# Gated-DeltaNet/Conformer mixer of a decoder step: the work between the recurrence's steps put into one pinned stream, its head in a pool of its own, tanh for sigmoid and silu, states updated on VectorE

## The chip, the cores and the metric

One core of one Trainium2 chip runs the whole program. The metric is the device time of one execution in microseconds (us), the median of three runs. TensorE is called PE here, VectorE DVE, ScalarE ACT, GpSimd POOL, SyncE SP, as in the profile.

## What is computed

One inference step of a two-layer decoder for 256 prompt tokens and 8 sample tokens, which share weights and stand side by side as T = 264 columns. The change concerns the first layer's mixer and the norms; the mixer cut to what matters is:

```python
proj = h @ p['ab_w_in']                       # q,k,v | z | b,a | ga,gb
qkv, new_dn_conv = causal_depthwise_conv(qkv_raw, dn_conv, p['dn_conv_w'])   # 4 taps
q, k, v = split(silu(qkv));  q = l2_normalize(q) * 128**-0.5;  k = l2_normalize(k)
beta = sigmoid(b_raw);  g = -exp(A_log) * softplus(a_raw + dt_bias)
o, new_S = gated_delta_rule(q, k, v, g, beta, dn_S)      # chunks of 64, 4 heads of 128
o = rms_norm(o, p['dn_norm_g']) * silu(z)
glu = ga * sigmoid(gb)
c, new_cc_conv = causal_depthwise_conv(glu, cc_conv, p['cc_conv_w'])         # 31 taps
c = silu(layer_norm(c + p['cc_conv_b'], p['cc_ln_g'], p['cc_ln_b']))
y = concatenate([o, c], -1) @ p['ab_w_out']
```

The delta rule needs, for each chunk and head, the inverse of a unit lower triangular 64x64 matrix. Every sample token has a state of its own, 4 heads of 128x128, that is decayed and gets an outer product of key and value. Around the mixer stand feed-forward layers, cross-attention to 256 memory tokens (whose keys and values are projected here too) and a layer norm after each.

## The kernel before

Activations lie transposed (channels on partitions, tokens in columns), and float32 products are made of three: a weight is split into `whi` (a cast on ACT, L224) and `wlo` (a subtraction on DVE, L217), and high times high, low times high and high times low are added. So a projection works by **units** of 128 output columns; a unit's 24 matmuls (8 blocks of 128 rows, 3 each) are called products (`Unit.products`, L700). Weights come in blocks of 128x8x256 ("raw", 1 MB, three buffers) on SP's queue.

The Tile framework's scheduler sets each engine's order by the program's dependences and the order of writing; an instruction marked by `pin` (`keep_in_program_order`) stays where it is written. An engine runs its list in order: an instruction that waits holds up all behind it.

The mixer (`mixer`, L868) goes through these steps:

- `Norm.finish` ends the feed-forward's norm while the query and key units are projected; `ev_qkv` (L911) copies each unit to `qkvraw` and makes the 4-tap convolution: an ACT multiplication (L916) and three DVE steps of 128x256 (L918). Sample tokens get their taps on POOL from transposed state rows (`conv_states`, tiles stn, dsn, dsT). Silu of four groups at once is at L934.
- **Head of the recurrence**: b and a are projected (`pba`), turned (`pbt`) and give beta and the decay gv by a chain of small ACT and DVE steps (L1006 to L1032). Sums of squares of keys and queries (`sq`, L1078 and L1081) give the l2 norms, `br2` and, after a Newton root (`rsqrt`, L125 to L131), `nk`. The running decay is spread by an all-ones product of `tg` = tri times gv (8 ACT multiplications, L1115, one matmul a chunk half, L1119); with it DT, NT (keys by keys) and AT (queries by keys) are made. The 256 tokens are two halves of 128, c = 0 and 1.
- **Levels**: five doubling levels (L1263 on) invert 32x32 blocks for both halves. In a level a half needs np (DVE), a product of X (L1278), a transposition of XP, a product of XT (L1286), a subtraction on DVE and four copies to X (L1247), each waiting for the one before. Two larger levels (32 to 64, 64 to 128) follow; then the halves are run through (`vn,XT`, L1350, to the state S). The sample tokens' states are read twice: once for key and query times state (`S_s,kq`, L1203), once in `update`.
- **What fills the gaps** is written after the recurrence: the gated units ga and gb (`glu`), the 31-tap convolution as 32 matmuls for each of 4 groups (`taps`, L972), the z units (`zeta`), `conv_norm`, and four units of the next attention's keys (`fill`). Nothing of that is pinned; the scheduler draws it forward into gaps that it foresees. The value units are projected ahead of the head.
- **End**: `update` multiplies each of 8 state blocks by its decay on ACT (L1464) and adds the outer product 128x512 at a time on DVE (L1469), four times; `og` is the normed output times z; then the output projection begins, whose first products need the split of `og` (xlo, L187).

ACT holds one set of function tables; an `ACT_TABLE_LOAD` stands where the next function is not in it. The mixer has ten.

## Time and profile before

| | us |
|---|---|
| three runs, lowest / median / highest | 1386.66 / 1388.01 / 1389.65 |
| the profiled execution | 1386.02 |
| its span, from first to last instruction | 1384.3 |
| PE busy in the span | 1345.3 (97%) |
| DVE busy | 938.5 (68%) |
| ACT busy | 747.5 (54%) |
| POOL busy | 200.1 (14%) |

The mixer lies between 248 us (the transposition of stn) and 408 us (the output projection's first product). "Busy" counts the time in which at least one instruction of the engine is under way; "granted clock" (PEclk) is the mean share of full speed in a stretch, and the clock has two levels, 2.4 and 1.2 GHz, so 0.90 is a fifth of the stretch at the lower one. In a timeline a row joins like instructions that follow each other: its start, its duration, their count, and in brackets how long the engine had been idle before and what ended the wait. Matmul records of float32 operands other than the split ones come twice for one matmul.

### The profile page before, as it was taken

To read this page: it belongs to the slowest core of one execution; us is meant where nothing else is said; L and a number is where in the kernel's file an instruction comes from. 1 tells how busy PE (TensorE), PEld (TensorE's weight loads), DVE (VectorE), ACT (ScalarE), POOL (GpSimd) and SP (SyncE) were. 2 spreads that over 40 slices of the span, in tenths; PEclk is the share of its full clock that TensorE was granted. 3 is DMA by queue.
4 is the path that set the end of the run, shared out by engine and by line. 5 is a ranking of instruction groups with operands and counts; after the bars stand their busy time and mean duration, and the time that the engine had idled before them with its cause. 6 is when DMAs were issued, how large, how long until landed. Compare 5 with 4: busy or idle time off the path is not lost. (4 is left out here: it accounts for less than half of the span.)

```text
span 1384.3 us, 27373 instructions
## 1 busy us (share of the span) xinstructions
PE 1345.3 (97%) x10959; PEld 1272.9 (92%) x10959; DVE 938.5 (68%) x1910; ACT 747.5 (54%) x1372; POOL 200.1 (14%) x242
## 2 busy tenths in 40 slices
PE   8999999988989999999999999999999999999998
PEld 8999999865879978999999999999999968999997
DVE  5555668865658776975556865556888987855554
ACT  4455447774555644664445654445766635744443
POOL 3312410301111000111121011121112001011021
PEclk9999999999989999999999999999999999999999
DMA  7654766436569988455556755555648993665551
GB/s 261 216 165 159 242 193 183 142 109 152 179 186 313 290 279 258 152 176 181 184 176 195 211 172 181 179 174 182 192 147 273 287 299 119 189 203 183 175 169 53
DMA packets 270543, 269.27 MB, mean 195 GB/s; under 512 B 8243, under 2 KB 266291, under 8 KB 270400
## 3 DMA queue, kind: packets, MB, share of 16 engines
q1 hardware_dynamic: 257392, 260.94, 59.7%
q10 hardware_dynamic: 13024, 6.59, 1.9%
q8 instruction: 86, 1.41, 0.4%
q14 instruction: 41, 0.34, 0.1%
HBM read 252.81 MB, written 15.26 MB: 194 GB/s over the span
## 5 line engine op out<-in xcount | busy, mean ns | idle before, releaser
L217 DVE TENSOR_TENSOR wlo<-raw,whi 128x1024 fp32r<-128x1024 f32 (+1 forms) x380 | 460.9, 1220 | 247.5 <-ACT whi L224 244.3
L224 ACT CAST whi<-raw 128x1024 fp32r<-128x1024 f32 (+1 forms) x380 | 389.1, 1030 | 412.9 <-PE mm L700 221.9
L700 PE MATMUL mm<-xhi,whi 128*128 128x264 f32 x1728 | 495.5, 288 | 5.3 <-ACT whi L224 5.2
L700 PE MATMUL mm<-xhi,wlo 128*128 128x264 f32 x1728 | 495.9, 288 | 3.2 <-DVE wlo L217 3.2
L700 PE MATMUL mm<-xlo,whi 128*128 128x264 f32 x1728 | 494.3, 287 | 0.1
L700 PEld LDWEIGHTS mm<-xhi,whi 128*128 128x128 f32 x1728 | 327.5, 190 | 10.1 <-ACT whi L224 6.7
L700 PEld LDWEIGHTS mm<-xhi,wlo 128*128 128x128 f32 x1728 | 326.4, 189 | 8.9 <-DVE wlo L217 4.4
L700 PEld LDWEIGHTS mm<-xlo,whi 128*128 128x128 f32 x1728 | 328.2, 190 | 2.9 <-issue 1.4
L857 PE MATMUL mm<-hh,whi 128*128 128x264 f32 x704 | 200.8, 285 | 0.0
L858 PE MATMUL mm<-hl,whi 128*128 128x264 f32 x704 | 200.4, 285 | 0.0
L859 PE MATMUL mm<-hh,wlo 128*128 128x264 f32 x704 | 200.1, 284 | 0.0
L857 PEld LDWEIGHTS mm<-hh,whi 128*128 128x128 f32 x704 | 132.6, 188 | 0.1
L858 PEld LDWEIGHTS mm<-hl,whi 128*128 128x128 f32 x704 | 132.3, 188 | 0.1
L859 PEld LDWEIGHTS mm<-hh,wlo 128*128 128x128 f32 x704 | 132.4, 188 | 0.0
L187 POOL TENSOR_TENSOR hl<-sg,hh 128x264 fp32r<-128x264 f32 x44 | 61.2, 1392 | 444.8 <-ACT hh L180 444.8
L700 PE MATMUL mm<-xpre,whi 128*128 128x266 f32 x640 | 117.1, 290 | 0.9 <-ACT x L455 0.6
L700 PEld LDWEIGHTS mm<-xpre,whi 128*128 128x128 f32 x640 | 97.9, 189 | 2.1 <-ACT x L455 0.7
L700 PE MATMUL mm<-xpre,wlo 128*128 128x266 f32 x320 | 85.1, 287 | 0.0
L380 POOL TENSOR_TENSOR lnQ<-lnQ,lnsq 128x264 f32<-128x264 f32 x40 | 40.5, 1012 | 298.3 <-ACT lnsq L373 298.2
L806 DVE TENSOR_TENSOR sg<-mm,sg 128x264 f32<-128x264 f32 x76 | 32.9, 432 | 51.3 <-PE mm L700 49.8
L700 PEld LDWEIGHTS mm<-xpre,wlo 128*128 128x128 f32 x320 | 57.7, 189 | 0.1
L1660 DVE CUSTOM_DVE_ANT_0 junk<-cache,ax 128x256 f32<-128x256 f32 x128 | 47.2, 412 | 4.8 <-PE ax L1655 4.6
(492 smaller groups left out, 1775.4 us busy)
## 6 DMA issues: line engine op xcount, KB each, us to landing
raw<-in_ffn_w_gate_dram SPq DMA_DIRECT2D x43, 1024.0 KB
raw<-in_ffn_w_up_dram SPq DMA_DIRECT2D x43, 1024.0 KB
raw<-in_ffn_w_down_dram SPq DMA_DIRECT2D x32, 1024.0 KB
cache<-in_cache_mem_k_dram SPq DMA_DIRECT2D x32, 512.0 KB
cache<-in_cache_mem_v_dram SPq DMA_DIRECT2D x32, 512.0 KB
raw<-in_ffn_w_down_dram SPq DMA_DIRECT2D x16, 768.0 KB
raw<-in_ab_w_in_dram SPq DMA_DIRECT2D x12, 1024.0 KB
raw<-in_xa_wk_dram SPq DMA_DIRECT2D x8, 1024.0 KB
```

The source lines that it names most:

```text
L187: e.tensor_tensor(out=lo, in0=src, in1=f32(hi), op=ALU.subtract)
L217: e.tensor_tensor(out=lo[:, :nk], in0=r, in1=f32(hi[:, :nk]), op=ALU.subtract)
L224: A.copy(hi[:, :nk], r)
L380: pin(e.tensor_tensor(out=Q, in0=Q, in1=sq, op=ALU.add), last)
L700: pin(PE.matmul(self.ps, lhsT=self.w[q // 2][:, k, :], rhs=self.rhs[q % 2][:, k, :], start=self.n == 1, stop=self.n == 3 * KT), pinned)
L806: V.tensor_tensor(out=sg, in0=pu, in1=sg, op=ALU.mult)
L857: PE.matmul(ps, lhsT=hi[:, k, :], rhs=xh, start=n == 0, stop=False)
L858: PE.matmul(ps, lhsT=hi[:, k, :], rhs=xl, start=False, stop=False)
L859: PE.matmul(ps, lhsT=lo[:, k, :], rhs=xh, start=False, stop=n == FT - 1)
L1660: V.tensor_tensor_reduce(out=junk, in0=kc[:, b, a, :], in1=pq[:, b * 256:(b + 1) * 256], scale=1.0, scalar=0.0, op0=ALU.mult, op1=ALU.add, ...
```

## The change

The changed mixer computes the same. `values`, `stream`, `f` and `TE` are new:

- A generator `stream` holds the four value units, gb and ga units, z units and the taps in a fixed sequence; `f(n)` takes the next n matmuls of it, and stands between the recurrence's steps. `TE` pins the recurrence's matmuls too, so PE's order from the head on is the written one.
- The head (ss, br2, DT, NT, AT, eG) moves ahead of the value units, with tiles in a pool `ge`. The values are turned (`values(c)`) in levels 1 and 2.
- In a level the first products of both halves stand together with 8 matmuls of the stream behind each, then the second products with 8 behind each.
- `pg` is made by 4 matmuls with gv broadcast as the stationary operand; the `tg` multiplications go. Sigmoid and the values' silu go by tanh (the conv weights are halved once, and one DVE step 128x1056 multiplies th + 1 by the halved value); gb gets a second ACT step. z's multiplication by dng on POOL is folded into DVE steps.
- A state is updated by 8 DVE steps of 128x128 that multiply by the decay and add the outer product; two of the four state blocks stay in the buffers of the first reading. `vb` is made by 8 ACT multiplications, before by 2 on POOL.
- `conv_norm` is filled with products of key units. Before, five key units were made in the mixer, one ahead of the head and four at the end; now four are, all at the end, and one (24 products and its transpositions) moves to the norm that ends the next attention.
- Small norm tiles become slices of two blocks of 128x3xT, which the taps' input uses later in place of a raw buffer. The raw loads that this frees go on SP's queue earlier: one stands ahead of the load of dsn.

```diff
+        class TE:
+            def matmul(*a, **k):
+                pin(PE.matmul(*a, **k))
...
-                if 1:
-                    o = qkv[i]
-                A.activation(out=o, in_=o, func=AF.Silu)
+                if i < 2:
+                    A.activation(out=o, in_=o, func=AF.Silu)
+                else:
+                    th = cp.tile([P, 4, T], F32, name="th")
+                    A.activation(out=th, in_=o, func=AF.Tanh)
+                    V.scalar_tensor_tensor(out=o, in0=th, scalar=1.0, in1=o, op0=ALU.add, op1=ALU.mult)
...
-            A.activation(out=gbt[n], in_=ps, func=AF.Sigmoid)
+            A.activation(out=gbt[n], in_=ps, func=AF.Tanh, scale=0.5)
+            A.activation(out=gbt[n], in_=gbt[n], func=AF.Identity, scale=0.5, bias=half)
...
+            seq = [(1024, 8, ev_qkv), (1280, 10, ev_qkv), (2056 + 512, 0, ev_gb), (2056, 0, ev_ga), (2056 + 768, 2, ev_gb), 10,
+                   (2056 + 256, 2, ev_ga), 11, (1536, 0, ev_z), 12, (1536 + 256, 2, ev_z), 13]
...
+        def f(n):
+            for _ in range(n):
+                next(fill_in, None)
...
-        fill(0, 1)
-        proj(ab_w_in, 1024, 4, rhs, lambda n, ps: ev_qkv(8 + n, ps))
...
         for c in range(2):
+            f(8 + 4 * c)
+            pg = ax_ps()
             for h in range(H):
-                if 'AAAAAAAA'[4 * c + h] == 'A':
-                    A.mul(tg[:, h, :], tri, gv[:, c, h:h + 1])
...
-            PE.matmul(pg, lhsT=ones[1], rhs=tg.rearrange("p h i -> p (h i)"), start=True, stop=True)
+                TE.matmul(pg[:, h * P:(h + 1) * P], lhsT=gv[:, c, h:h + 1].broadcast_to([P, P]), rhs=tri, start=True, stop=True)
...
         for l in range(5):
...
                     A.copy(xt, pt[:, :P])
-                    px = ax_ps()
...
+                f(8)
+            for c in range(2) if l else ():
+                px = ax_ps()
+                for b in range(4):
+                    TE.matmul(px[32 * b:32 * b + 32, :P], lhsT=xts[c][:, 32 * b:32 * b + 32], rhs=XT[c][:, b, :], start=True, stop=True)
+                V.tensor_tensor(out=XP[c], in0=XP[c], in1=px[:, :P], op=ALU.subtract)
                 spread_blocks('VVVV', X[c], XP[c])
...
+                f(8)
+            if l in (1, 2):
+                values(l - 1)
...
-            S_s = gp.tile([P, 8, P], F32, tag="S_s", name="S_s2", bufs=2)
-            A.dma_start(S_s, S_in[:, 8 * g:8 * g + 8, :])
-            for i in range(8):
-                A.mul(S_s[:, i, :], S_s[:, i, :], eb[:, 0, 2 * g + i // 4, i % 4:i % 4 + 1])
+            S_s = held[g]
+            if g < 2:
+                S_s = gp.tile([P, 8, P], F32, tag="S_s", name="S_s2", bufs=2)
+                A.dma_start(S_s, S_in[:, 8 * g:8 * g + 8, :])
...
-                V.tensor_tensor(out=S_s[:, 4 * a:4 * a + 4, :], in0=S_s[:, 4 * a:4 * a + 4, :], in1=hd(po), op=ALU.add)
+                for h in range(4):
+                    V.scalar_tensor_tensor(out=S_s[:, 4 * a + h, :], in0=S_s[:, 4 * a + h, :], scalar=eb[:, 0, 2 * g + a, h:h + 1],
+                                           in1=hd(po)[:, h, :], op0=ALU.mult, op1=ALU.add)
...
+        keys = kv_units(0, 4)
+        conv_norm(Filler(keys))
+        for n in range(2):
+            update(n)
```

ACT's order has four table loads in the mixer (ten before). PE's order counts as follows, from the transposition of stn to the output projection's first product (products of the 16 projected units, products of key units, taps):

| stretch of the program | before | after |
|---|---|---|
| stn to the first product of pg | 216 products, 24 key products | 48 products |
| pg to the first level's first product | 4 products | 65 products |
| there to `vn,XT` | 110 products, 64 taps | 148 products, 32 taps |
| there to the end of the recurrence (`pr,ones` of the sample tokens) | 6 products, 17 taps | 27 products, 5 taps |
| there to the output projection | 48 products, 47 taps, 96 key products | 96 products, 91 taps, 96 key products |

**ACT, from the silu of keys and queries (tiles keys and mixs) to the squares of the queries.** Before, in two pieces:

```order
L934 ACTIVATE keys<-keys 128x1056
L934 ACTIVATE mixs<-mixs 128x1056
L1006 ACT_TABLE_LOAD
L1006 ACTIVATE beta<-BA 128x12
L1012 ACTIVATE se<-sx 128x12
```

```order
L934 ACT_TABLE_LOAD
L934 ACTIVATE mixs<-mixs 128x1056
L944 ACT_TABLE_LOAD
L944 ACTIVATE gb<-mm 128x264
L1078 ACTIVATE sq<-keys 128x512 x2
L1177 ACT_TABLE_LOAD
L1177 ACTIVATE egs<-gv 8x4
L1078 ACTIVATE sq<-mixs 128x512 x2
```

After, in one:

```order
L954 ACTIVATE keys<-keys 128x1056
L954 ACTIVATE mixs<-mixs 128x1056
L1127 ACTIVATE sq<-keys 128x512 x2
L224 CAST whi<-raw 128x1024
L1080 ACTIVATE beta<-BA 128x12
L1085 ACTIVATE se<-sx 128x12
L937 COPY qkvraw_2573<-mm 128x264
L1086 ACT_TABLE_LOAD
L1086 ACTIVATE se<-se 128x12
L1088 ACTIVATE eA<-eA 128x4
L938 ACTIVATE mixs<-mm,par 128x256
L1093 ACT_TABLE_LOAD
```

The squares stand right behind the silu of keys and queries; the first value unit's cast and copy stand between the steps of the decay's chain, and the values' silu has left this stretch.

**DVE, the last part of the head, up to the first level's np.** Before:

```order
L1142 COPY wl<-DT 128x4
L1150 TENSOR_TENSOR vn<-ax,nk 128x512 x2
L1126 TENSOR_TENSOR DT<-ax,mneg 128x512
L1144 TENSOR_TENSOR eG<-eG,mixs 128x512
L1266 TENSOR_TENSOR np<-NP,pmask 128x128
L1169 TENSOR_SCALAR kq_3593<-ax 128x64
L1273 TENSOR_TENSOR np<-id_101,np 128x128
```

After (mixs is here the value tile; th its tanh):

```order
L1175 SCALAR_TENSOR_TENSOR NT<-ax,br_3293,DT 128x128 x4
L1182 TENSOR_TENSOR AT<-ax,DT 128x512
L1184 COPY wl<-DT 128x4
L217 TENSOR_TENSOR wlo<-raw,whi 128x1024
L940 SCALAR_TENSOR_TENSOR mixs<-qkvraw_2573,par,mixs 128x256 x3
L959 SCALAR_TENSOR_TENSOR mixs<-th,mixs 128x1056
L1231 COPY kq<-keys 128x32
L1232 COPY kq<-mixs 128x32
L1248 TENSOR_TENSOR dg<-ident,beta 8x32
L1235 TENSOR_TENSOR kq_3571<-kq 128x64
L1238 TENSOR_SCALAR kq_3571<-ax 128x64
L1337 TENSOR_TENSOR np<-NP,pmask 128x128
```

The values' convolution, their silu and a weight's low part now stand ahead of np; vn has moved behind it.

**PE, the end of the mixer** (o_nat is the recurrence's output, csq the conv norm's squares, vb,k the outer products of the states). Before:

```order
L1392 MATMUL mm<-mixs,ones_86 128x264 x4
L1428 MATMUL ax<-ident,o_nat 128x128 x8
L1450 MATMUL ax<-ident,kv_4959 128x128 x2
L1399 MATMUL mm<-ones_80,csq 128x1 x12
L1468 MATMUL ax<-vb,k_4971 128x512 x8
L140 MATMUL mm<-dg,ones_80 128x264
```

After:

```order
L710 MATMUL mm<-mlo,whi 128x256
L710 MATMUL mm<-mhi,wlo 128x256
L887 MATMUL ax<-vb,k_4475 128x512 x4
L740 MATMUL mm<-ident,kvT 128x128 x4
L1554 MATMUL ax<-ident,o_nat 128x128 x3
```

The output's transposition, ahead of the conv norm's squares before, now stands behind the last outer products and the key units.

## Rows read from the trace of the kernel before

**Rows 1.** The profile's page, part 1: busy time of PE, its share of the span, instructions.

```profile
PE 1345.3 (97%) x10959; PEld 1272.9 (92%) x10959; DVE 938.5 (68%) x1910; ACT 747.5 (54%) x1372; POOL 200.1 (14%) x242
```

**Rows 2.** The mixer in stretches: from and to in us, length, then busy time (and count of instructions) of PE, PEld, DVE, ACT and POOL, the granted clock, the DMA engines' share and GB/s; the last line adds them up.

```profile
248.00:264.00 16.00, 14.31 (x118) 12.06 (x117) 13.76 (x31) 10.38 (x21) 8.75 (x20) 0.90 0.25 77
264.00:283.00 19.00, 18.58 (x150) 17.92 (x148) 14.45 (x37) 16.64 (x28) 3.98 (x8) 1.00 0.66 201
...
290.00:303.00 13.00, 8.42 (x53) 6.32 (x52) 11.10 (x44) 11.79 (x30) 1.05 (x2) 0.95 0.15 44
303.00:330.00 27.00, 23.84 (x286) 16.05 (x290) 21.88 (x81) 15.14 (x46) 2.47 (x3) 0.90 0.33 90
330.00:352.00 22.00, 18.55 (x299) 14.68 (x290) 3.96 (x22) 8.87 (x24) 2.32 (x3) 0.84 1.04 246
352.00:365.00 13.00, 13.00 (x129) 10.75 (x130) 8.70 (x28) 9.03 (x34) 0.97 (x1) 1.00 0.01 2
...
376.00:391.00 15.00, 12.03 (x59) 8.44 (x58) 11.73 (x31) 4.53 (x11) 5.39 (x4) 0.75 0.72 219
391.00:409.00 18.00, 15.28 (x111) 14.10 (x109) 7.36 (x15) 11.81 (x31) 1.95 (x4) 0.92 0.53 153
sum 161.00, PE 141.81 PEld 114.24 DVE 101.66 ACT 97.26 POOL 27.83; mean PE 14.18 PEld 11.42 DVE 10.17 ACT 9.73 POOL 2.78
```

**Rows 3.** PE's timeline at the borders of the mixer's steps: start in us, duration, engine, line, operation, count, idle time before and what ended it.

```profile
248.52 0.37 PE L893 MATMUL ax<-ident,stn 120*128 120x120 f32 x2
...
283.02 0.43 PE L1081 MATMUL ax<-sq,ones 128*32 128x128 f32 x8 [0.38 <-ACT sq L1078]
...
290.18 0.59 PE L1119 MATMUL ax<-tg,ones 128*128 128x512 f32 x1
...
303.65 0.66 PE L1278 MATMUL ax<-X,np 128*32 128x128 f32 x8 [1.11 <-DVE np L1266]
...
329.48 0.42 PE L1286 MATMUL ax<-XT,xt 128*32 128x128 f32 x8 [0.29 <-ACT xt L1283]
...
330.59 1.91 PE L972 MATMUL mm<-cinx 128*32 128x256 f32 x32
...
338.36 0.64 PE L1203 MATMUL ax<-S_s,kq 128*32 128x128 f32 x16 [1.03 <-DMA S_s<-in_state_dn_S_dram]
...
352.29 0.38 PE L1350 MATMUL ax<-vn,XT 128*128 128x128 f32 x1
...
364.41 0.31 PE L1225 MATMUL ax<-pr,ones 128*128 128x32 f32 x2
...
408.40 0.37 PE L700 MATMUL mm<-xhi,whi 128*128 128x264 f32 x1
```

**Rows 4.** What PE waited for between 248 and 409 us: the line that waits and what ended the wait, total in us, times, longest.

```profile
PE mm L700 <- ACT whi L224: 3.3, 2, 1.7
PE ax L1203 <- DMA S_s<-in_state_dn_S_dram: 3.1, 2, 2.0
...
PE ax L1286 <- ACT xt L1283: 1.8, 6, 0.3
PE ax L1278 <- DVE np L1266: 1.8, 2, 1.1
PE ax L1468 <- DVE S_s L1469: 1.5, 1, 1.5
```

**Rows 5.** ACT's timeline around the silu of keys and queries, and at the squares of the queries.

```profile
261.56 1.08 ACT L934 ACTIVATE keys<-keys 128x1056 f32<-128x1056 f32 x1 [3.94 <-POOL keys L931]
262.55 1.07 ACT L934 ACTIVATE mixs<-mixs 128x1056 f32<-128x1056 f32 x1
263.63 1.28 ACT L1006 ACT_TABLE_LOAD   x1
264.93 0.21 ACT L1006 ACTIVATE beta<-BA 128x12 f32<-128x12 f32 x1
...
284.91 1.14 ACT L1078 ACTIVATE sq<-mixs 128x512 f32<-128x512 f32 x2
...
287.35 0.59 ACT L1083 COPY st<-ax 128x512 f32<-128x512 f32 x1 [1.31 <-PE ax L1081]
```

**Rows 6.** Groups by line between 248 and 409 us, the last two of ACT and the others of DVE: line, engine, operation, tiles, shapes, count, busy us, mean ns of one, idle time before and what ended it.

```profile
L217 DVE TENSOR_TENSOR wlo<-raw,whi 128x1024 fp32r<-128x1024 f32 x21 | 26.6, 1278 | 4.8 <-ACT whi L224 4.8
L918 DVE SCALAR_TENSOR_TENSOR mixs<-qkvraw,par,mixs 128x256 f32<-128x256 f32 x24 | 10.8, 481 | 0.1
...
L1469 DVE TENSOR_TENSOR S_s<-S_s,ax 128x512 f32<-128x512 f32 x8 | 5.3, 678 | 0.9 <-ACT S_s L1464 0.9
...
L1134 DVE SCALAR_TENSOR_TENSOR NT<-ax,br,DT 128x128 f32<-128x128 f32 x8 | 2.4, 350 | 0.2 <-ACT DT L1128 0.2
...
L1150 DVE TENSOR_TENSOR vn<-ax,nk 128x512 f32<-128x512 f32 x2 | 1.4, 688 | 1.3 <-PE ax L1148 1.3
...
L224 ACT CAST whi<-raw 128x1024 fp32r<-128x1024 f32 x20 | 20.6, 1048 | 8.5 <-PE mm L700 4.7 <-DMA raw<-in_xa_wk_dram 3.8
...
L916 ACT ACTIVATE mixs<-mm,par 128x256 f32<-128x256 f32 x4 | 1.9, 482 | 0.0
```

**Rows 7.** PE in a stretch of the following attention, where the moved key unit goes (columns as in Rows 2).

```profile
452.00:465.00 13.00, 13.00 (x110) 13.00 (x110) 7.25 (x12) 8.79 (x14) 0.00 (x0) 1.00 0.93 296
```

**Rows 8.** SP's queue: the issue of the load of dsn.

```profile
251.78 0.34 SPq L899 DMA_DIRECT2D dsn<-in_state_dn_conv_dram  x1
```

More of the change, by code (lines that the diff above doesn't have):

```diff
@@ L275, in turn, with block @@
         return PE.matmul(ps[:, k % 4 * P:(k % 4 + 1) * P], lhsT=t, rhs=ident, start=k % 4 == 0, stop=False, is_transpose=True)
+    def block(name, i):
+        t = work.tile([P, 3, T], F32, tag=f"nb{i}", name=name, bufs=1)
+        return [t[:, j, :] for j in range(3)]
     class Norm:
@@ L969, in taps @@
+        def taps(n, xs, w8):
             pv = mm_ps()
@@ new lines, in mixer @@
+        st = ge.tile([P, 512], F32, tag="AT0", name="st")
+        A.copy(st, pss)
+        f(8)
+        pss = ax_ps()
+        for m in range(4):
+            TE.transpose(pss[:, m * P:(m + 1) * P], st[:, m * P:(m + 1) * P], ident)
+        V.tensor_scalar(out=ss, in0=pss.rearrange("p (i c h r) -> p i c h r", i=2, c=2, h=H)[:, :, :, :, 0], scalar1=1e-6, scalar2=None, op0=ALU.add)
+        br2 = ge.tile([P, 2, H], F32, name="br2")
+        V.reciprocal(out=br2, in_=ss[:, 0])
+        V.tensor_tensor(out=br2, in0=br2, in1=beta[:, 0:2, :], op=ALU.mult)
@@ L1158, in mixer @@
         smp = {}
+        held = {}
         def sample_step():
```

435 lines of the change are left out of this document (232 added, 203 removed).

## The prediction

> **What bounds the kernel now.** I read the page first: PE is busy 97% of the span [rows 1], so a change can gain only where PE idles or runs at the lower clock. The stretches of the mixer show where: of 161.0 us between 248 and 409 PE is busy 141.8, so it idles 19.2, and the granted clock falls to 0.90, 0.84 and 0.75 in stretches around the recurrence [rows 2]. A stretch of 22 us at 0.84 has lost (1 - 0.84) x 22 = 3.5 us of full speed if PE was busy in its slow part; so counted, the stretches shown lost some 13 us in all. Then the border times [rows 3] give five segments: stn to pg 41.7 us (248.5 to 290.2), pg to the first level 13.5, there to `vn,XT` 48.6, there to the end of the recurrence 12.1, there to the output projection 44.0; 159.9 in all. Last the waits [rows 4]: the largest are for weights' casts (3.3) and for the samples' states from DMA (3.1, in front of `S_s,kq`); xt and np, steps within a level, cost 1.8 each. In the first stretches PE is nearly full (18.58 of 19.00), in pg to the first level it is not (8.42 of 13.00), and there DVE is (11.10 of 13.00) [rows 2].
>
> A product costs PE 13.00/110 = 0.118 us where it is full [rows 7], and a tap matmul 1.91/16 = 0.12 (32 records are 16 matmuls) [rows 3]; I take 0.12 for both.
>
> **The change, segment by segment.** PE's work is first moved: 192 products leave segment 1 (240 to 48), -23.0 us; 61 enter segment 2, +7.3; in segment 3 38 more products and 32 fewer taps, +0.7; in segment 4 +21 and -12, +1.1; in segment 5 +48 products and +44 taps, +11.0. The sum is -24 products, the key unit that goes to the attention. What the waits do beside that decides.
>
> *Segment 1, stn to pg.* PE loses what filled it; the end is then set by ACT. The silu of keys waits for POOL as before (3.94 us, starting 261.56), the queries' silu ends at 262.55 + 1.07 = 263.6 [rows 5]. Behind it ACT has in its order: squares of keys 1.14, a cast 1.05 [rows 6], beta and abs 0.2 each, the first value unit's copy (264 columns, where st's 512 take 0.59) 0.4, a table load 1.28, two small exponentials 0.2 each, the unit's convolution step 0.48 [rows 6], a second load 1.28, Ln 0.2, squares of queries 1.14: 7.8, so 271.4. From there PE needs the sums of squares, 16 products (1.9, partly beside), the copy st 0.59 [rows 5] and two transposing steps: 2.6. pg starts at 274.0; the segment has 25.5 us, -16.2. Bounds: 272.5 if the scheduler's pieces fall beside each other, 278.5 if dsn arrives later (its load, issued at 251.78 [rows 8], now stands behind a 1 MB weight load) and the emptied PE falls to the lower clock.
>
> *ACT tables.* Six loads go: by the row of one load, 1.28 with the next activation 0.02 behind its end (263.63 to 264.93) [rows 5], 6 x 1.28 = 7.7 us of ACT, most of it beside PE's work; I count none of it separately. The Trainium skill ("ScalarE: Activation LUTs", section "What ACT_TABLE_LOAD costs") puts a switch at about 2.66 us, load and drain together; the trace shows no such drain, and by the page the two loads left in the head would put pg 2.8 us later than I say.
>
> *Segment 2, pg to the first level.* DVE sets it: 11.10 busy of 13.00 now [rows 2], in a chain. The order puts ahead of the first level's np three low parts at 1.28 (3.8), nine convolution steps of the values at 10.8/24 = 0.45 (4.1), the values' silu step of 1056 columns (not in the trace; twice the 512 columns of 0.68, so 1.3), and takes two vn out (-1.4) [rows 6]: +7.8. The tanh that the silu step waits for stands on ACT ahead of the copies NP, about 1.1 as a silu of the same size [rows 5], and some 0.9 of DVE's 1.9 idle us fills up: 21.5 us, +8.0. Bounds: 18 if most of DVE's added steps fall in waits that the chain has anyway, 25 if each waits for its cast. The four matmuls of pg in place of one (0.59 [rows 3]) and the tg multiplications that go change this by a few tenths either way.
>
> *Segment 3, levels to `vn,XT`.* Four levels with products take 25.8 us now (303.65 to 329.48 [rows 3]); DVE is busy 21.9 of 27 there [rows 2]. It gets some 1.6 more low parts (2.0) and the two vn (1.4): 25.3. PE gets 28 more matmuls (3.4) and loses most of the waits for xt and np. I take 27, with DVE nearly the bound: +1.2. The rest, 22.8 us now, has 21 fewer products (-2.5) and loses the lower clock of 330 to 352 (-3.5) if PE is kept busy before it. The wait for the states, 3.1 [rows 4], I keep for the most part: there are two buffers, so the third and fourth block can be asked for only when the first two have been read, as now, and the next taps' input is loaded at the same time; -1.1. A new one comes: the states' turned products stand right behind their copy on ACT (sT, 512 columns, as st 0.59 [rows 5]), where 16 taps stood between; twice, +1.3. So 17.0, the segment 44.0, -4.6. Bounds: 38 and 49.
>
> *Segment 4.* +1.1 of work, and the seams of eight matmuls wait for vnew and S1 on DVE and ACT: I add 1.3 for two such waits (a 512-column step 0.68 each [rows 6]); 14.5, +2.4, between +1 and +4.
>
> *Segment 5.* Now 44.0. PE idles 3.0 and 2.7 in its last two stretches, and the clock there (0.75 and 0.92) has lost 3.75 and 1.4 [rows 2]: 10.9 that could go (the wait of 1.5 for S_s on DVE [rows 4] is in it), about as much as the 11.0 of work that comes. But new waits come. The output's split stands behind 16 state updates of 128x128 on DVE, 16 x 0.35 = 5.6 us where 4 x 0.68 stood [rows 6], and og, two steps of 512 columns; the first products of the output projection need it, and PE has only 2 to 3 us of transpositions and outer products beside it: 3. vb, now eight ACT steps, has ten taps (1.2) to cover it: 1. So 48.2, +4.2, between 0 and +8. The state multiplications that leave ACT, the two state loads that go and POOL's dng lay beside PE's work: nothing, unless ACT's casts there come sooner.
>
> *The attention* gets 24 products, 2.9, and two transpositions, 0.2. PE is full there (13.00 of 13.00 [rows 7]), so all of it counts: +3.1.
>
> Sum: -16.2 + 8.0 - 4.6 + 2.4 + 4.2 + 3.1 = -3.1. The profiled execution took 1386.0 (its span 1384.3 and 1.7 around it), so it would take 1382.9; the median of the runs stands 2.0 above it, which gives **1384.9**. The rest of the kernel, the norms with their two blocks among it, I leave unchanged: the tiles are the same size, and PE is full beside them.
>
> **The rivals.**
>
> *PE becomes the bound from the first level on* (bigger gain): the two halves' steps overlap so well that DVE's low parts fall between them. Segment 2 at 19.5, segment 3 at 40.0, segment 4 at +1.5, segment 5 at +2.0: -16.2 + 6.0 - 8.6 + 1.5 + 2.0 + 3.1 = -12.2, so 1375.8. For it: DVE was idle 18 of 22 us between 330 and 352 [rows 2], so its work can be spread. Against: in segments 2 and the levels the order holds DVE's steps fixed.
>
> *The waits only move* (the stream does fill the recurrence, but what it fills with was not idle time in the head): the head is a chain on ACT, DVE and POOL with 48 products to cover 25 us, and PE idles there instead. If pg starts at 278.5, segment 1 gains 11.7 in place of 16.2: sum +1.4, so 1389.4, no change. For it: POOL's 3.94 and the ACT chain cannot be shortened by PE's order; against: half of the chain is counted from rows already.
>
> *DVE's order makes it slower*: PE's order is now fixed, so a product whose low part is late holds up the level behind it, where the scheduler before could slip in other work; and DVE has a low part of 1.28 us between the chain's small steps. If a level takes 8.0 us in place of 6.75 (+5.0) and segment 2 24.0 (+2.5), the sum is +4.4, so 1392.4. With that segment 2 it is measurably slower from a level of 7.6 on. For it: DVE at 25.3 of 27 by my own count; against: a level at 6.5 now with DVE 81% busy and the lower clock for a fifth of it.
>
> **How the numbers follow.** The forecast, from -7 to 0 (1381 to 1388), gets 0.42; the larger gain 0.18; waits that only move 0.17; slower 0.23. A measurement of this kernel tells about 0.2% (2.8 us) from no change, so below 1385.2 is faster and above 1390.8 slower. Of the forecast two thirds lie below 1385.2: faster 0.28 + 0.18 = 0.46; same 0.14 + 0.17 = 0.31; slower 0.23. Cases of both signs hold much of the chance, so the range reaches to both: the segments' bounds, taken together at half their widths, go some 10 us either way, 1374 to 1394, and about 0.1 lies on each side (a late head with slow levels above; no new waits in segments 3 and 5 with a quick head below).
>
> **What would show it.** In the changed profile: pg at 274 (278 for the rival of moved waits); the first level's X,np at 295.5, `vn,XT` at 339.5, the end of the recurrence at 354, the output projection at 402. DVE nearly full from pg to the end of the levels, PE's waits there named as np, XP or wlo. A wait of 1 to 3 us for the states in front of `S_s,kq`, and two near 0.6 for sT. In segment 5 a wait of several us for og's low part. If the granted clock is below 0.9 in the head as well as in the levels, I am wrong on the slow side; if levels take 6 us, on the fast side.

## The result, and the profile after

The changed kernel takes 1404.99 us (median of 4 runs, 1402.19 to 1406.38) beside 1388.18 of the kernel before: the ratio is 1.0126, interval 1.0111 to 1.0140. It is 17 us slower where 3 us less were forecast, and above the range. The profiled execution took 1402.19, its span 1400.5.

The stretches between the same border points as before (from the first transposition of stn to pg, the first level's product, the states' first product, `vn,XT`, the end of the recurrence, and the norm after the output projection; columns as in [rows 2]):

```profile
247.40:277.40 30.00, 17.31 (x130) 13.69 (x129) 19.33 (x52) 16.02 (x32) 9.17 (x21) 0.72 0.28 84
277.40:299.10 21.70, 15.32 (x133) 14.59 (x134) 19.17 (x60) 13.21 (x33) 3.63 (x8) 0.95 0.36 107
299.10:328.40 29.30, 28.11 (x275) 22.06 (x275) 22.46 (x80) 17.11 (x51) 0.43 (x1) 0.92 0.48 134
328.40:346.50 18.10, 14.64 (x286) 11.55 (x286) 4.86 (x21) 8.26 (x23) 3.11 (x4) 1.00 0.62 180
346.50:359.50 13.00, 13.00 (x111) 12.06 (x110) 10.15 (x33) 4.30 (x16) 0.00 (x0) 1.00 0.09 26
359.50:448.20 88.70, 80.72 (x660) 68.29 (x660) 55.66 (x148) 39.99 (x78) 6.80 (x13) 0.94 0.68 210
sum 200.80, PE 169.10 PEld 142.25 DVE 131.63 ACT 98.89 POOL 23.14; mean PE 28.18 PEld 23.71 DVE 21.94 ACT 16.48 POOL 3.86
```

The kernel before, counted at the same borders (first and last stretch, and the sum of all six):

```profile
248.52:290.18 41.66, 39.53 (x336) 35.41 (x335) 29.27 (x76) 31.83 (x59) 12.73 (x27) 0.96 0.49 147
...
364.41:437.54 73.13, 67.05 (x523) 58.06 (x522) 51.59 (x124) 39.29 (x81) 13.59 (x14) 0.93 0.79 248
sum 189.02, PE 169.62 PEld 140.63 DVE 125.74 ACT 115.27 POOL 33.13; mean PE 28.27 PEld 23.44 DVE 20.96 ACT 19.21 POOL 5.52
```

PE idles 31.7 of the 200.8 us, where before it idled 19.4 of 189.0: it is busy as long as before (169.1 and 169.6) and idles 12.3 more. The head (first row) has 17.3 busy of 30.0 at a granted clock of 0.72, where before 41.7 us there were nearly full (39.5) at 0.96; pg to the first level 15.3 of 21.7 at 0.95. The levels (third row) are nearly full: 28.1 of 29.3. The last row, 88.7 us, has 8.0 idle and a clock of 0.94; before it was 73.1 with 6.1 idle at 0.93.

Where PE waits between 248 and 425 us, to be read against [rows 4]:

```profile
PE ax L924 <- DMA dsn<-in_state_dn_conv_dram: 5.9, 1, 5.9
PE ax L887 <- ACT sq L1127: 5.6, 2, 5.0
PE ax L887 <- DVE np L1337: 3.7, 2, 3.0
PE ax L887 <- DVE kq L1235: 3.3, 1, 3.3
PE mm L710 <- DVE kvn L741: 2.7, 2, 2.1
PE mm L887 <- DMA cinx<-cin: 2.4, 2, 1.8
PE ax L890 <- ACT sT L1276: 1.8, 2, 1.1
...
```

Of the waits of [rows 4] those for weights' casts, for states from DMA and for xt are gone, and that for the state update is down from 1.5 to 0.9. In their place stand waits of the head: for dsn and for the squares; between pg and the first level for kq and np; and at the end for kvn and for the taps' input (cinx). On PE's timeline, against [rows 3]:

```profile
255.70 1.45 PE L924 MATMUL ax<-ident,dsn 24*128 24x24 f32 x12 [5.92 <-DMA dsn<-in_state_dn_conv_dram]
...
272.20 1.18 PE L887 MATMUL ax<-sq,ones 128*32 128x128 f32 x16 [5.01 <-ACT sq L1127]
...
277.44 0.83 PE L887 MATMUL ax<-tri,gv 128*128 128x128 f32 x6
...
299.06 0.66 PE L887 MATMUL ax<-X,np 128*32 128x128 f32 x8 [3.05 <-DVE np L1337]
...
346.54 0.38 PE L887 MATMUL ax<-vn,XT 128*128 128x128 f32 x2
...
359.55 0.31 PE L887 MATMUL ax<-pr,ones 128*128 128x32 f32 x2
...
419.40 0.36 PE L710 MATMUL mm<-xhi,whi 128*128 128x264 f32 x1 [2.06 <-DVE kvn L741]
```

dsn's load lands where it did, but nothing lies before its transposition now: 5.92 us. The squares of the queries are waited for 5.01 us; pg starts at 277.44. `X,np` waits 3.05 for np and starts at 299.06. `vn,XT` comes at 346.54 (before 352.29), the recurrence ends at 359.55 (364.41). The output projection begins at 414.99 (408.40) with twelve products of the convolution's half, after 0.68 us for a copy kvn (the copy that empties a key unit's accumulator), and waits for another one, 2.06 us, at 419.40.

ACT in the head, against [rows 5]:

```profile
263.62 1.08 ACT L954 ACTIVATE keys<-keys 128x1056 f32<-128x1056 f32 x1 [6.04 <-POOL keys L951]
264.61 1.07 ACT L954 ACTIVATE mixs<-mixs 128x1056 f32<-128x1056 f32 x1
265.58 1.13 ACT L1127 ACTIVATE sq<-keys 128x512 f32<-128x512 f32 x2
...
271.54 1.13 ACT L1127 ACTIVATE sq<-mixs 128x512 f32<-128x512 f32 x2
...
273.45 0.59 ACT L1132 COPY st<-ax 128x512 f32<-128x512 f32 x1 [0.78 <-PE ax L887]
```

The silu of keys starts 2.1 us later than before, again behind POOL. POOL's first step behind the copy dsT, before and after:

```profile
257.33 0.55 POOL L929 TENSOR_TENSOR keys<-dsT,par 128x32 f32<-128x32 f32 x1 [2.33 <-ACT dsT L903]
...
257.73 3.15 POOL L949 TENSOR_TENSOR keys<-dsT,par 128x32 f32<-128x32 f32 x1 [5.17 <-ACT dsT L925]
```

The step starts 0.4 us later and takes 2.6 us more; why it does, no run shows. From the end of the silu of queries (265.68) to the end of the squares of the queries (272.67) ACT runs 7.0 us without a wait, through the steps that the prediction counted at 7.8.

### The profile page after: what moved, and what is told of

It is laid out like the page before. It is cut to its first block, busy times and chain, and to the rows that moved or that the text cites. A ratio compares the mean times of both kernels' runs of the same rounds, so it can differ in the third digit from the quotient of the medians.

```text
span 1400.5 us, 27426 instructions
## 1 busy us (share of the span) xinstructions
PE 1348.5 (96%) x10971; PEld 1277.9 (91%) x10971; DVE 945.7 (68%) x1937; ACT 732.8 (52%) x1338; POOL 190.9 (14%) x239
## 5 line engine op out<-in xcount | busy, mean ns | idle before, releaser
L867 PE MATMUL mm<-hh,whi 128*128 128x264 f32 x704 | 200.8, 285 | 0.0
L869 PE MATMUL mm<-hh,wlo 128*128 128x264 f32 x704 | 200.1, 284 | 0.0
L385 POOL TENSOR_TENSOR lnS<-lnS,lnsq 128x264 f32<-128x264 f32 x40 | 40.0, 1000 | 299.5 <-ACT lnsq L378 299.4
```

The costliest lines, as they stand in the source:

```text
L385: pin(e.tensor_tensor(out=Q, in0=Q, in1=sq, op=ALU.add), last)
L867: PE.matmul(ps, lhsT=hi[:, k, :], rhs=xh, start=n == 0, stop=False)
L869: PE.matmul(ps, lhsT=lo[:, k, :], rhs=xh, start=False, stop=n == FT - 1)
```

## The experiments

Each is the changed kernel with one edit, unless it says otherwise; times are ratios to the kernel before of the same session. One caution on places: the program from the first attention's scores to the end, which no experiment's edit touches, took between 899.9 and 904.4 us in the profiled executions. So differences under some 4 us count here only where the intervals part, and a single trace's place counts only for what is in that place. And the profiled execution of the changed kernel is the fastest of its four (1402.2, its median 1405.0), so a run's gain by its median can be some 3 us more than its places show.

| run | ratio | interval | median us | stn to the norm behind the mixer, us |
|---|---|---|---|---|
| before | 1 | | 1387.2 to 1388.2 | 189.0 |
| changed | 1.0126 | 1.0111 to 1.0140 | 1405.0 | 200.8 |
| e1 dsn early | 1.0126 | 1.0107 to 1.0144 | 1404.4 | 197.0 |
| e2 key unit in head | 1.0064 | 1.0048 to 1.0081 | 1396.9 | 200.0 |
| e3 output early | 1.0097 | 1.0081 to 1.0114 | 1401.7 | 200.9 |
| e4 no pins | 0.9912 | 0.9898 to 0.9927 | 1374.8 | 173.9 |
| e5 stream free | 0.9953 | 0.9937 to 0.9970 | 1381.2 | 179.5 |
| e6 recurrence free | 1.0066 | 1.0046 to 1.0085 | 1396.5 | 196.5 |
| e7 head filled | 1.0047 | 1.0029 to 1.0064 | 1393.9 | 192.5 |
| e8 no pins, e2, e3 | 0.9900 | 0.9884 to 0.9915 | 1373.4 | 175.5 |
| e9 no pins, old update | 0.9907 | 0.9890 to 0.9924 | 1374.5 | 173.5 |
| e10 no pins, no tanh | 0.9928 | 0.9909 to 0.9947 | 1378.6 | 176.7 |
| e11 pins, e2, e3, filled | 1.0030 | 1.0018 to 1.0042 | 1392.0 | 192.1 |
| e12 e8 with dsn early | 0.9930 | 0.9908 to 0.9952 | 1378.1 | 181.1 |
| e13 products without use | 1.0076 | 1.0059 to 1.0093 | 1399.0 | 200.1 |
| e14 keys first | 1.0070 | 1.0055 to 1.0085 | 1398.3 | 197.6 |

### Waits of the head and the end, one by one: e1, e2, e3

```diff
-            dsn = cp.tile([NS * 3, 1536], F32, tag="stn", name="dsn")
-            SP.dma_start(dsn, state_dn_conv.rearrange("b t c -> (b t) c"))
...
+        dsn = cp.tile([96, 512], F32, name="dsn")
+        G.memset(dsn, 0.0)
+        for a in range(3):
+            SP.dma_start(dsn[32 * a:32 * a + 24, :], state_dn_conv.rearrange("b t c -> (b t) c")[:, a * 512:(a + 1) * 512])
```

> The changed kernel with one edit: the 24 state rows dsn get a tile of their own (three blocks of 24 rows, turned by 4 transpositions in place of 12) and their load is issued ahead of that of stn, so that it need not wait for stn's tile nor stand behind a 1 MB weight load. Theory A (the head of the recurrence lost its cover: 192 products left it and PE now stands idle or at the lower clock there): the wait of 5.92 us in front of the transposition of dsn goes, the silu of keys comes 3 to 5 us earlier, pg at about 273 to 275 in place of 277.4, time 3 to 5 us under the changed kernel (about 1400 to 1402). Theory B (the pinned order of products and recurrence is what costs): the head's wait is replaced by another of nearly the same length, gain under 1.5 us.

The ratio is that of the changed kernel. PE's timeline of this run shows why, in two of its rows between 250 and 264 us:

```profile
251.68 0.52 PE L927 MATMUL ax<-ident,dsn 96*128 96x96 f32 x4 [0.28 <-issue]
...
263.01 1.16 PE L887 MATMUL ax<-id,ba 128*128 128x8 f32 x6 [6.89 <-DVE ba L1071]
```

The wait for dsn is gone, and the next pinned matmul, which turns the copied b and a, waits 6.89 us for that copy: on DVE the copy stands behind twelve convolution steps and two weights' low parts. So the silu of keys came 5.3 us earlier (258.31), but pg only 2.0 (275.45), and the median does not tell it: a chain in a fixed row passes a wait on to its next member. (The profiled execution took 1399.2, 5 us under the run's median, so its 197.0 in the table is not to be set against that; and the runs spread over 7.6 us, so a gain of 2 us is not excluded.)

```diff
+            hf = kv_units(0, 1)
+            Filler(hf).products(24, True)
             pt = ax_ps()
             for ct in range(12):
-                PE.transpose(pt[:, ct * 24:(ct + 1) * 24], dsn[:, ct * P:(ct + 1) * P], ident[:24, :24])
+                TE.transpose(pt[:, ct * 24:(ct + 1) * 24], dsn[:, ct * P:(ct + 1) * P], ident[:24, :24])
             A.copy(dsT, pt[:, :288].rearrange("p (c n) -> p c n", c=12))
+            hf[0].finish()
```

> The changed kernel with one edit: the key unit that the change moved to the attention (24 products and two transpositions) is put back into the mixer, pinned between the transposition of stn and that of dsn. Theory A: PE idles 7 us there, so the 2.9 us of products are free in the head and go from the attention, and PE has the higher clock a little longer: 3 to 5 us less than the changed kernel (1400 to 1402), the wait for dsn shrinks from 5.9 to about 3. If the attention was not full there, or the head moves back by what is put in: under 1 us.

The 24 products cost the head nothing (stn to pg 29.3 us in place of 30.0) and are missing from the attention (40.5 us from the norm to the scores, changed 42.8, before 40.1). The median fell by 8 us, more than was expected and more than the 3 that the places show; the profiled executions of the two kernels differ by those 3.

```diff
+        f(10000)
+        for c in range(2):
+            pt = ax_ps()
...
-        for c in range(2):
-            pt = ax_ps()
...
```

> The changed kernel with one edit: the recurrence's output (transposition of o_nat, og, its split) is made right behind the stream's end, ahead of the conv norm and of the last two state updates. Theory A' (at the end of the mixer 16 state updates of 128x128 on DVE stand ahead of the output's split, and PE waits for it at 411 to 419 and then runs at the lower clock): idle of PE between 410 and 427 falls by 3 us or more, time 3 to 6 us less (1399 to 1402). Against it: the split moves DVE work into the conv norm's chain, which then ends later by as much, gain under 1.5 us.

The block from the transposition of o_nat to the split of og and os_ was moved whole. The interval touches that of the changed kernel, and the mixer is no shorter in the trace (200.9): nothing is shown. o_nat was turned at 375.8 in place of 411.7, and from the end of the recurrence to the norm PE still waited 2.3 us for a copy kvn, so the split of og alone was not what the end waited for.

### The pins: e4, e5, e6

```diff
             def matmul(*a, **k):
-                pin(PE.matmul(*a, **k))
+                PE.matmul(*a, **k)
             def transpose(*a):
-                pin(PE.transpose(*a))
+                PE.transpose(*a)
...
-                        u.products(1, True)
+                        u.products(1)
```

> The changed kernel with one edit: the recurrence's matmuls and the stream's products and taps are no longer pinned to the written order, so that the scheduler orders them as it does in the kernel before. Theory A (missing cover in the head, displaced work at the end): the order written is near what the scheduler makes, within 4 us of the changed kernel either way (1401 to 1409). Theory B (the pinned order costs): 8 us or more less, near the kernel before (1388 to 1397).

30 us less than the changed kernel, and faster than the kernel before, ratio 0.9912. The same stretches:

```profile
248.90:277.90 29.00, 24.22 (x197) 20.90 (x195) 22.35 (x52) 18.73 (x39) 9.86 (x22) 0.88 0.41 123
277.90:297.10 19.20, 18.32 (x155) 17.55 (x155) 17.39 (x63) 14.60 (x34) 3.23 (x8) 1.00 0.36 99
297.10:321.80 24.70, 23.97 (x289) 16.57 (x293) 20.14 (x76) 15.65 (x49) 0.20 (x2) 1.00 0.79 218
321.80:336.80 15.00, 15.00 (x286) 10.93 (x274) 8.10 (x30) 6.72 (x19) 2.58 (x2) 1.00 0.60 168
336.80:349.30 12.50, 12.50 (x111) 11.33 (x111) 7.38 (x26) 5.74 (x19) 0.19 (x2) 1.00 0.48 141
349.30:422.80 73.50, 68.39 (x568) 58.29 (x567) 52.66 (x147) 36.09 (x73) 8.11 (x11) 0.98 0.78 242
sum 173.90, PE 162.40 PEld 135.57 DVE 128.02 ACT 97.52 POOL 24.17; mean PE 27.07 PEld 22.60 DVE 21.34 ACT 16.25 POOL 4.03
```

The head takes 29.0 us, as with the pins, but in it PE is busy 24.2 us in place of 17.3: the scheduler put 115 products ahead of pg where the written order has 48. pg to the first level is full (18.3 of 19.2), the clock is 1.00 from pg to the end of the recurrence. In all 11.5 us idle in place of 31.7, and the last row is 73.5 us: what ran in the head no longer stands behind the recurrence.

From stn to the norm 15.1 us are gone against the kernel before, and the attention takes 42.7 for 40.1 with its additional key unit: 12.5 in all, in accord with the median (12.7).

In e5 only the stream is free, in e6 only the recurrence:

```diff
-                        u.products(1, True)
+                        u.products(1)
...
-                    TE.matmul(pv[32 * g:32 * g + 32, :NP], lhsT=w8
+                    PE.matmul(pv[32 * g:32 * g + 32, :NP], lhsT=w8
```

```diff
-                pin(PE.matmul(*a, **k))
+                PE.matmul(*a, **k)
...
-                    TE.matmul(pv[32 * g:32 * g + 32, :NP], lhsT=w8
+                    pin(PE.matmul(pv[32 * g:32 * g + 32, :NP], lhsT=w8
```

> The changed kernel with the stream's products and taps not pinned, the recurrence's own matmuls still pinned among themselves. If what costs is that the stream holds fixed places (theory B1: too few products where the chain waits long, as in the head with 48, and products in front of steps that are ready), this alone brings most of the gain of the run without pins: time 1373 to 1382. If the recurrence's own fixed order costs (B2, a half that is ready waits behind one that is not), the time stays above 1395.

> The changed kernel with the recurrence's matmuls not pinned, but the stream's products and taps pinned among themselves. Their order among themselves is the one that their weights come in, so under B1 (the places between the recurrence's steps cost, not the stream's own sequence) this too brings most of the gain, 1373 to 1384, because a sequence pinned alone may still slide against the recurrence. If the stream's own sequence costs (taps that wait for their input hold up the z products behind them: B3), it stays at 1390 or more.

The stream's free places alone bring 24 of the 30 us, the recurrence's 8 alone. e5 and e4 are the same up to the end of the recurrence, to 0.1 us in each stretch (29.1, 19.1, 24.7, 15.0, 12.5), and differ in the last, 79.0 to 73.5. There the pinned outer products of the states (`update`) and what follows them still hold on to their row; that these are the 5.5 us is likely, no run frees them alone. In e6 the gain lies in that last stretch too (82.4), while the states' products to `vn,XT` took 2.1 us more (20.2 for 18.1). So what costs up to the end of the recurrence is the stream's fixed places, as B1 has it, and the recurrence's own row costs only at the end.

### More products in the head, the pins kept: e7, e11, e13

```diff
+            f(36)
             pt = ax_ps()
             for ct in range(12):
-                PE.transpose(...)
+                TE.transpose(...)
...
         for i, t in enumerate((kk, q)):
+            if i:
+                f(24)
             for c in range(2):
```

> The changed kernel, all pins kept, with two calls more of the stream in the head: 36 products between the transpositions of stn and of dsn, 24 between the squares' sums of keys and of queries; so 108 products stand ahead of pg in place of 48 (the scheduler, let free, put 115 there). Under B1 the head's idle of 12 us takes them for nothing: pg within 1.5 us of 277.4, time 7 to 11 us less (1394 to 1398); the rest of the 30 us must then lie in the levels and the end. If the pins cost by something else than by missing cover in the head, pg moves back by 5 us or more and the gain is under 3 us.

60 products more in the head, and it takes 29.7 us in place of 30.0; the time falls by 11 us, as B1 has it. So 8 us of the loss by the trace, 11 by the median, are products that the written order put behind the head although the head had room for them. What is left against the run without pins, 19 us, lies in the levels (30.8 us, there 24.7) and in the last stretch (84.9, there 73.5).

e11 has the edits of e2 and e3, `f(24)` behind the key unit's products and `f(24)` between the squares.

> All pins kept, but better numbers: the key unit back in the head (24 products), two more calls of the stream there of 24 each, the output's split ahead of the conv norm. If the loss is one of numbers (cover in the head) and of the end's order, the three gains add up, less what the head has no more room for: 12 to 18 us under the changed kernel (1387 to 1393), near the kernel before. If they overlap (all three take the same idle time), 1393 or more. It should not reach the run without pins (1375), because the levels' runs of eight stay.

13 us under the changed kernel, above the kernel before: the lower end of what was expected, the gains overlap. Its head has 120 products (96 of the stream, 24 of the key unit) and its mixer 192.1 us; the last stretch is 84.4, where the run without pins has 73.5.

> The changed kernel, all pins kept, with 60 products in the head whose result nothing reads (36 between the transpositions of stn and dsn, 24 between the two pairs of squares' sums); nothing of the work is moved or left out. The run with 60 products of the stream at the same places gained 11 us, of which 7.2 are the products themselves (60 x 0.12), that no longer stand behind. If the other 4 are the higher clock that a busy PE keeps there (0.72 in the head of the changed kernel, 0.89 with the products), then these products, useless for the result, gain 2 to 5 us (1400 to 1403). If the gain was the moved work alone, this is no faster than the changed kernel, 1404 to 1408.

```diff
-            f(36)
+            dps = ax_ps()
+            for n in range(36):
+                TE.matmul(dps[:, :T], lhsT=rhs[0][:, 1, :P], rhs=rhs[0][:, 0, :], start=n == 0, stop=n == 35)
```

This is against e7, and `f(24)` likewise. The granted clock of the head rose to 0.94:

```profile
248.10:276.56 28.46, 21.68 (x190) 18.31 (x189) 19.77 (x52) 15.99 (x32) 9.64 (x21) 0.94 0.30 90
276.56:298.44 21.88, 15.50 (x130) 14.72 (x128) 19.09 (x60) 13.23 (x33) 3.63 (x8) 0.90 0.35 105
```

The head took 28.5 us (changed 30.0). From stn to the end of the squares of the queries it is as long as in the changed kernel (25.3 and 25.2), for there ACT, DVE and POOL set it; the gain is in PE's own steps behind the squares, 3.1 us for 4.8. From stn to the norm nearly nothing is left of it (200.1, changed 200.8), since the last stretch took 90.1 for 88.6. So the higher clock in the head is worth some 1.6 us there, and of the 8.3 us by which e7's mixer is shorter, useless products at the same places bring 0.7: e7's gain is the moved work.

The median is 6 us lower all the same, below both ranges that were expected. 2.8 of the 6 are that the changed kernel's profiled execution lies that far under its median; the profiled executions differ by 3.5, and the traces put 3.9 into the part that nothing touches (899.9 us, changed 903.8). There the two differ in two places of the second layer. The changed kernel first, then e13, at either place:

```profile
1109.65 3.45 PE L1763 MATMUL ax<-atts,qT 128*128 128x256 f32 x8 [1.13 <-DMA atts<-kT]
1108.85 1.99 PE L1770 MATMUL ax<-atts,qT 128*128 128x256 f32 x8
...
1184.85 0.59 PE L710 MATMUL mm<-xhi,wlo 128*128 128x264 f32 x1 [2.42 <-DVE wlo L217]
1182.60 0.39 PE L710 MATMUL mm<-xhi,wlo 128*128 128x264 f32 x1 [2.42 <-DVE wlo L217]
```

In front of the attention's scores the changed kernel waits 1.13 us for kT from DMA, the granted clock falls to 0.5 (its lower level, 1.2 GHz), and the scores take 3.45 us in place of 1.99. Behind the wait of 2.42 us, which both have, the clock falls to 0.5 in the changed kernel and stays at 1.00 in e13. What the products in the head should have to do with either, no run shows.

### The end: e14

```diff
+        for u in keys:
+            u.place = mm_ps
+            u.finish()
         for n in range(2):
             update(n)
-        for u in keys:
-            u.place = mm_ps
-            u.finish()
```

> The changed kernel with one edit: at the end the key units' transpositions and their copies kvn stand ahead of the last two state updates in place of behind. The output projection waits 2.7 us for a copy kvn, which frees the accumulator that its products need and stands on DVE behind 16 state updates and og; PE then runs at the lower clock for some 5 us. If that is the end's loss: that wait goes and the time is 2 to 5 us less (1400 to 1403). If the split of og is what is waited for in any case, under 1.5 us.

7 us less by the median, the mixer 3.2 us shorter in the trace, and 3.1 between the two profiled executions. What PE waited for longest from the end of the recurrence on:

```profile
PE mm L887 <- DMA cinx<-cin: 2.7, 2, 2.0
PE ax L887 <- ACT vb L1495: 0.7, 1, 0.7
PE mm L710 <- ACT xhi L180: 0.6, 1, 0.6
PE mm L740 <- ACT kvT L732: 0.6, 1, 0.6
...
```

The two waits for kvn (2.7 us) are gone. They were waits for an accumulator: the key units' turned products lay in the pool from which the output projection takes its sums, and the copies that empty it stood on DVE in the changed kernel behind the 16 state updates. The first (PE waited 0.68 us) stood right behind them; the second (2.06 us) behind og, a weight's low part and half of og's split too, and waited itself 0.85 us for the DMA that carries an earlier kvn out. So the place of these copies in DVE's order is what the end waited for; moving og and its split alone (e3) left the wait.

### Parts of the change without the pins: e9, e10, e8, e12

e9 is e4 with the old `update`; e10 is e4 with

```diff
-            A.activation(out=gbt[n], in_=ps, func=AF.Tanh, scale=0.5)
-            A.activation(out=gbt[n], in_=gbt[n], func=AF.Identity, scale=0.5, bias=half)
+            A.activation(out=gbt[n], in_=ps, func=AF.Sigmoid)
...
-        A.activation(out=beta, in_=BA[:, :, 0:4], func=AF.Tanh, scale=0.5)
+        A.activation(out=beta, in_=BA[:, :, 0:4], func=AF.Exp, scale=-1.0)
```

and silu for the values; e8 is e4 with the edits of e2 and e3, e12 is e8 with that of e1.

> The run without pins, with the state update as it was: all four blocks loaded, each state multiplied by its decay on ACT (8 x 0.39 us a block) and the outer product added on DVE 512 columns at a time. If the update in one DVE step is one of the parts that gain (fewer waits of outer product on update, two loads less), this is 2 to 5 us slower than the run without pins (1377 to 1380). If its 16 DVE steps ahead of the output cost what they save, it is within 1.5 us of 1374.8; my prediction counted them as a loss of 3 at the end, by which it would be faster.

No difference: with ACT's multiplications and DVE's 512-column sums back, and two loads of states more, the time is the same (1374.5 and 1374.8). In the free order the state update is worth nothing that the runs can tell either way.

> The run without pins, with sigmoid, exp and silu in place of tanh (gb by sigmoid in one step, beta by exp and reciprocal, the values' silu in one ACT step, the conv weights not halved): five table loads of 1.28 us more on ACT in its order, one DVE step of 1056 columns less. By the rows of the loads 6 us of ACT more, of which those in the chain from the silu of keys to the first level count: 2 to 5 us slower than the run without pins (1377 to 1380). By the Trainium skill's figure (ScalarE: Activation LUTs, What ACT_TABLE_LOAD costs) of 2.66 us for each switch up to 13 us slower. If ACT is covered by products there: within 1.5 us.

Sigmoid, exp and silu in place of tanh: the intervals of e4 and e10 overlap (0.9898 to 0.9927 and 0.9909 to 0.9947). The median is 3.8 us higher and the mixer 2.8 longer, most of it between the levels and `vn,XT` (18.6 us for 15.0), while the head is 1.4 shorter. By the intervals 13 us more, the expectation's upper figure, is excluded; a few are likely but not shown.

> A version that may beat both: no pins on stream and recurrence, the key unit back in the mixer's head, the output's split ahead of the conv norm. The run without pins has little idle left in the head (it put 115 products there), so the key unit should bring less than the 8 us that it brought with the pins: 0 to 4 us; the early split 0 to 2, since there the scheduler drew it forward by itself. Together 1369 to 1375.

The best run, 0.9900, not to be told from e4. The attention is 2.4 us shorter (40.3 for 42.7) and stn to the norm 1.6 longer: with its head full, the mixer takes back most of what the key unit saves in the attention.

> The version of the run e8 (no pins, key unit in the head, output's split early) with the early load of dsn. With the pins the early load brought nothing, because pba and its copy behind twelve convolution steps of DVE stood in one fixed row with it. Without pins: pg comes up to 4 us earlier and the time is 1370 to 1373 if the head is bound by the chain from dsn; the same as e8 (1373.4) within 1.5 us if PE is full in the head anyway or DVE's convolution sets the silu.

No better than e8, rather worse, by 4.6 us of the medians with intervals that overlap; neither branch of the expectation. In its profiled execution, 4.5 us above the run's median, pg came 1.6 us earlier than in e8, and in the mixer a weight's low part (3.0 us, in e8 1.8) and the states' load (2.3, in e8 none) were waited for instead. The chain from dsn is not what binds the free version.

## Why the prediction was wrong

The work moved as the counts said: the records of the trace have, stretch by stretch, the products and taps of the table in the part on the change. What failed is the account of the waits beside it, and most of all one term of segment 5: the 10.9 us of idle and slow clock that "could go" there beside 11.0 us of new work. From the end of the recurrence to the norm no idle time went, 6.1 us became 8.0.

The span grew by 16.2 us where -3.1 was forecast. The difference of 19.3 is segment 1 with +4.5, segment 3 +3.5, segment 4 -1.5, segment 5 +7.2, the stretch from the output projection to the norm +4.1, which the sum had no term for, the rest of the kernel +2.9, and small terms (stn's earlier start -1.1, the attention -0.4, segment 2 +0.1).

- **Segment 1** (forecast 25.5, measured 30.0). The chain from silu to the squares was counted nearly rightly (7.8, measured 7.0), but not that it starts later (silu of keys 263.62 in place of 261.56) and that PE's own steps behind the squares take 4.8 us in place of 2.6; e13 shows them at 3.1 with the higher clock. stn began 1.1 earlier, so pg came 3.4 late. The deeper fault is that I took the leaving of 192 products for a gain of 23.0 with +6.8 of idle (measured: the head 11.7 shorter), and did not ask whether more products could have stayed there for nothing. e7 shows that 60 could, with the head no longer.
- **Segment 2** (forecast 21.5, measured 21.6): right, and set by DVE (busy 19.2 of 21.7), as the waits for kq and np say.
- **Segment 3** (forecast 44.0, measured 47.5). Levels 29.4 for 27: PE is the bound there, busy 28.1, not DVE (22.5), and its clock stayed at 0.92. The rest took 18.1 for 17.0: the wait for the states in front of `S_s,kq` went altogether, sT cost 1.8 where 1.3 was counted.
- **Segment 4** (forecast 14.5, measured 13.0): no seam waited.
- **Segment 5** (forecast 48.2 to the output projection's first product, measured 55.4; and to the norm behind it 73.1 became 88.6, +15.5 where +4.2 was forecast). This is the step that failed most. I set 10.9 us of idle and slow clock as what the moved work would fill. Up to the projection's first product 5.8 us of idle at a clock of 0.88 became 5.7 at 0.94, so some 2 us of slow clock went and no idle; and behind it, where PE had been full (0.3 idle at 1.00), stand 2.3 us of idle at 0.95. The new work brought its own waits (2.4 for the taps' input, 0.7 for vb, 2.7 for kvn), and nearly all of the products that came were added whole. The wait at the end was expected for the split of og; it was for kvn (the 16 state updates themselves took 4.2 us, not 5.6), since the projection begins with the convolution's half, which needs no og, but does need a free accumulator.
- **The attention** (+3.1): the norm to the scores went from 40.1 to 42.8, and back to 40.5 with the unit in the head; right.
- **The rest of the kernel, left unchanged**: from the scores to the end 900.8 became 903.8, within what this part varies; 0.5 of it comes right behind the scores, the rest, some 2.5, at the scores of the second layer's attention.

Of the rivals, "the waits only move" had the mechanism, PE idle in the emptied head, and the head's length (11.7 us shorter, as measured), but a price too small (1.4 in place of 17), because it left segments 3 and 5 at their forecasts. The slower rival had the cause, a fixed order of PE, in the wrong place: a level took 7.3 us, under the 7.6 from which it should decide, and DVE was not the bound. Neither asked what the same program would do with its order left to the scheduler, the question that separates the parts: without the pins the change gains 12.7 us, with them it loses 17.

What stays open: which part of the free version's gain belongs to the head's move and which to the two halves of a level standing side by side, and why POOL's first step in the head became longer. That the update (e9) has none of the gain beyond what the runs can tell is shown, that the tanh has little is likely.

## What to carry to other kernels

In a pinned stream, count the products that stand beside the head of a chain, where it waits longest, and not only those between its steps, and add products there until the chain moves (60 here, for 8 to 11 us). When a change brings both new code and a fixed order, measure it without the pins first: here the same code was 1% faster than before without them and 1% slower with them. And idle time that "could go" when work comes is no term of a sum before the new work's own waits are counted, the release of accumulators by a copy on a busy engine among them.

## What the runs showed of the hardware

The granted clock of a head with 17.3 us of work in 30.0 was 0.72, with 21.7 in 28.5 (useless products between) 0.94, and the head became 1.5 us shorter. The lower clock cost that little because up to the end of the squares the head took as long in either run (25.2 and 25.3 us), set by ACT, DVE and POOL; it cost only where PE's own steps behind them were waited for (4.8 us and 3.1).

The part of the program behind the mixer, which no experiment touches, took 899.9 to 904.4 us over sixteen profiled executions, more than the 0.2% that I took for what can be told. Its length goes with the granted clock. All sixteen executions wait the same 2.4 us for the same weight's low part in the second layer: in e4 and e13 the granted clock stays at its full level there and through the whole part (900.0 and 899.9 us); in the other fourteen it falls around that wait. Where it falls once and shortly, in the kernel before, e8 and e11, the part takes 900.8 to 901.0 us; with longer or further stretches at the lower level, 901.8 to 904.4. The same wait in the same instructions can thus bring the lower clock or not. Where PE also waits for kT before the second attention's scores, 1.1 us in the changed kernel, 1.0 in e12 and 0.8 in e7, the part takes 903.8 to 904.4.
